# A block up product in the second layer's MLP, the last two groups of the output projection as one product, and the entry's low parts on VectorE

## The chip, the cores and the metric

The kernel runs on one core of one Trainium2 chip. The metric is the device time of one execution in microseconds (us); less is better. The core's engines work side by side, each through its own list of instructions in a fixed order: TensorE (PE in the profile) multiplies, VectorE (DVE), ScalarE (ACT) and GpSimd (POOL) compute on tiles, SyncE (SP) issues the transfers from and to DRAM. An instruction waits for the tiles it reads, and for those it overwrites to be free.

## The reference, cut to what matters

Two layers over 1104 columns (tokens): 1024 new ones, 64 sample ones, 16 meta rows. Layer 0 is a Mamba mixer with eight groups and an MLP; layer 1 is sliding-window attention and an MLP, which no longer need the meta rows (1088 columns).

```
def rmsnorm(x, w):
    return x * lax.rsqrt(jnp.mean(x * x, axis=-1, keepdims=True) + EPS) * w

def sq_relu_mlp(h, norm_w, w_up, w_down):        # 1024 -> 4096 -> 1024
    return h + jnp.square(jax.nn.relu(rmsnorm(h, norm_w) @ w_up)) @ w_down

# layer 0
h = h + gated_group_rmsnorm(y, z, gate_w) @ w_out        # w_out: 2048 -> 1024
h = sq_relu_mlp(h, mlp_norm_w[0], w_up[0], w_down[0])
# layer 1
h = h + attention(h) @ w_o
h = sq_relu_mlp(h, mlp_norm_w[1], w_up[1], w_down[1])
y = rmsnorm(h, final_norm_w)
```

## The kernel before

**Precision.** Every float32 operand of a matmul is split into a high part (a cast to float32r on ScalarE) and a low part (the difference). A product of 128 by 128 weights is three matmuls (`mm3`: L151 high by high, L152 high weights by low activations, L153 low by high). `wunit` loads weights and splits them: cast L136 on ScalarE, low part L137 on GpSimd, and with `pre` a scaling L134 on GpSimd before.

**Columns** are handled in three chunks of one PSUM bank: 384, 384 and 336 (`CH`), in the second layer 384, 384 and 320 (`CH1`). Activations lie feature by partition: eight tiles u (or k) of 128 features. `S` holds the high and low parts of the eight tiles.

**Layer 0, end of the mixer.** `gate_group(g)` makes the gated and normed output of group g, `down` multiplies it by `w_out[g]` and adds the product to the stream `hh` (L695), group after group. In the last group the chunks are finished one by one in the order 0, 2, 1, and `done` of `entry` squares each pair of tiles (L769, sums L772, L775) and, after the last, takes the norm: the statistic is a matmul with ones (`sum_over`, cast `msh` L194, low part `msl` L195, matmuls L196 and L197), Ln and Exp on ScalarE (L205, L206), eight scalings (L782), eight casts (L783), eight low parts (L784), every other one on GpSimd.

**Layer 0, up product.** The 32 weight columns tiles are 16 pairs. Pair 0 is multiplied plainly (`plain_up`). For the other 15 the product of two by two blocks is formed with seven products instead of eight (Strassen and Winograd): `up_weights` makes the sums of weight blocks (`s`: L857, L863; their parts L847 on ScalarE, L848 on GpSimd), `sides` makes the differences of activation blocks (L793, in place) and their parts (casts L803, low parts L806 in two halves, one on GpSimd and one on VectorE). Six of the differences' part tiles lie in pool `T`. `up_pair` multiplies in the PSUM banks ma, md, mc, mb, ma, mc, md (`CHAIN`), 24 matmuls of 276 columns each time, joins them (L875) and writes the squared result to DRAM (`r_d`). Three of the eight steps of `sides` are issued ahead of the plain pair.

**Layer 0, down product.** `down_blocks` reads r back in eight blocks of four tiles, each loaded while the one before is multiplied; `parts` splits them (L926, L927). Tiles `hh` are loaded again from `h_d`.

**Layer 1.** Keys, values and queries, 64 attention blocks (scores in PSUM tiles `sc`, of which there are two) and four sample halves, then `out_unit`: product with `w_o`, two residual adds (L1304, L1305), cast (L1306) and low part (L1307) into `S`, squares (L84, sums L85). `finish` takes the three statistics together after the last output. The MLP is `mlp`: weights scaled by the norm's weight (L134), plain products, 24 matmuls per 128 columns of weights and chunk, the norm's factor applied at the eviction (L738). Its result stays in SBUF, four weight columns at a time, and goes straight into the down product.

**The order.** A list scheduler orders all instructions of an engine by a simulated timeline; tile pools with few buffers limit how far one engine runs ahead of another. A weight's raw tile has two buffers, its split parts six.

Of the kernel before, what the change touches and what calls it, by code (L numbers as in the profile page):

```python
# [8 lines left out]
F32 = mybir.dt.float32  # L9
# [7 lines left out]
P = 128  # L17
# [12 lines left out]
G = 8  # L30
# [10 lines left out]
QW = T // 4  # L41
# [3 lines left out]
class Norm:  # L45
# [30 lines left out]
    def squares(self, c, u, h):  # L76

        k, nc, n = self.k, self.k.nc, self.chs[c][1]
        if u == 0:
            self.acc[c] = k.n1("acc")[:, :n]  # L80
            nc.scalar.activation(out=self.acc[c], in_=h, func=AF.Square)
            return
        sq = k.n1("sq")[:, :n]
        nc.scalar.activation(out=sq, in_=h, func=AF.Square)  # L84
        nc.vector.tensor_tensor(out=self.acc[c], in0=self.acc[c], in1=sq, op=ALU.add)  # L85

    def finish(self, order):

        k, nc = self.k, self.k.nc
        self.rs = self.acc  # L90
        mss = {c: k.sum_over(self.rs[c], self.chs[c][1]) for c in order}
        for c in order:
            nc.scalar.activation(out=self.rs[c], in_=mss[c], func=AF.Ln, bias=k.eps1)
        for c in order:
            nc.scalar.activation(out=self.rs[c], in_=self.rs[c], func=AF.Exp, scale=-0.5)

# [16 lines left out]

class Kernel:
# [13 lines left out]
    def wunit(self, view, a, b, pre=None):  # L128
# [6 lines left out]
        wh, wl = (self.wtile([P, a, b]) for _ in range(2))  # L135
# [32 lines left out]
    def more_banks(self, ctx, n, stat=1):  # L168
        pool = self.pool("psx", bufs=n, space=PSUM, ctx=ctx)
        sp = self.pool("pss", bufs=stat, space=PSUM, ctx=ctx)  # L170
        old = self.gring
        self.gring = old + [pool] * n
        self.pstat = (sp, "ms", stat)
# [12 lines left out]
    def sum_over(self, ssum, n):  # L186
# [9 lines left out]
        nc.tensor.matmul(out=ms[:, :n], lhsT=self.ones_r, rhs=hi, start=True, stop=False)  # L196
# [3 lines left out]
    def rstd(self, ssum, n, eps, scale=1.0, rs=None):  # L200

        nc = self.nc
        if rs is None:
            rs = self.n1("rs")[:, :n]
        nc.scalar.activation(out=rs, in_=self.sum_over(ssum, n), func=AF.Ln, bias=eps, scale=scale)  # L205
        nc.scalar.activation(out=rs, in_=rs, func=AF.Exp, scale=-0.5)  # L206
        return rs
# [515 lines left out]
    def mlp(self, layer, hts, chs, mp, xs, tail, done, pre=None, first=None):  # L723
        nc, i = self.nc, self.i
        for fb in range(8):
            rx = {}
            for c in range(len(chs)):
                rh = mp.tile([P, 4, 384], F32R, tag="rh", bufs=3, name="rh")
# [881 lines left out]
```

## Time and profile before

| | |
|---|---|
| median of 3 runs | 3107.47 us (3106.71 to 3111.19) |
| the profiled execution | 3105.48 us |
| its span in the trace | 3103.8 us |
| mean granted clock of TensorE | 0.981 |
| PE busy | 2956.5 us, 18862 matmuls |
| VectorE, ScalarE, GpSimd busy | 1806.4, 1251.5, 1261.7 us |
| DMA | 258.31 MB, mean 83 GB/s |

The page of the profile has the busy time of each engine, the span in 40 slices of 77.6 us with the busy share in tenths, the chain of work that ended last (PE makes 79% of it), and groups of instructions by line. A view of waits says which instruction waited for which and how long; the windows view gives the same busy times for a stretch of the span. Duration of a single matmul includes the overlap with the next one, so the rate of a stage is read from how many start in a window. The stages in time: mixer until about 1080, the first MLP's up product until about 1470, its down product until about 1690, keys, queries and attention until 2288, its last outputs until 2311, the second MLP until the end.

### The profile page before, as it was taken

The page shows a single profiled execution, that of the slowest core. Times are in us where ns is not written, and L with a number is a line of the kernel's source. Part 1 is how long each engine was busy: PE and PEld are TensorE (multiplying, and loading weights), DVE is VectorE, ACT ScalarE, POOL GpSimd, SP SyncE. Part 2 cuts the span into 40 slices and gives each one's busy share as a digit, 9 for nine tenths or more (in the row PEclk, how much of TensorE's full clock was granted, in tenths as well). Part 3 has the DMA queues.
Part 4 walks back from the last instruction along what each step waited for, and adds up shares of the span by engine and source line. Part 5 has one row for each costly group of instructions (what it writes and reads, how often), then busy time and mean ns, then how long its engine had stood idle before and what let it go on. Part 6 is the DMA issues. An engine that isn't in the chain of part 4 may idle for free.

```text
span 3103.8 us, 47669 instructions
## 1 busy us (share of the span) xinstructions
PE 2956.5 (95%) x18862; PEld 2828.9 (91%) x18862; DVE 1806.4 (58%) x3113; ACT 1251.5 (40%) x2425; POOL 1261.7 (41%) x1054
## 2 busy tenths in 40 slices
PE   6999999989999959999999999999979999999998
PEld 4988889879999959999999998888869999999998
DVE  5777777775656684333433356787976543344436
ACT  5455555554544555444211126665642111111113
POOL 4466666653323254444212145575542223222222
PEclk8999999999999979999999999999999999999999
DMA  3244444444212213333422212122111111111111
GB/s 128 67 121 116 119 125 117 131 123 139 66 61 73 99 53 103 110 113 129 170 102 71 77 41 62 63 85 89 62 48 41 46 44 48 42 48 41 48 41 65
DMA packets 165351, 258.31 MB, mean 83 GB/s; under 512 B 25656, under 2 KB 122040, under 8 KB 163064
## 3 DMA queue, kind: packets, MB, share of 16 engines
q1 hardware_dynamic: 165128, 255.27, 26.4%
q8 instruction: 148, 2.42, 0.3%
q14 instruction: 75, 0.61, 0.1%
HBM read 207.55 MB, written 48.63 MB: 83 GB/s over the span
## 4 chain that ended last, share of the span: by engine, by line
PE 79%; DVE 10%; ACT 4%; issue 3%; POOL 2%; DMA 2%; SPq 0%; DVEq 0%; POOLq 0%; ACTq 0%
PE g L152 20%; PE g L151 20%; PE g L153 20%; PE y L565 1%; PE mc L153 1%; PE mc L151 1%; PE mc L152 1%; PE md L152 1%; PE md L153 1%; PE md L151 1%; PE ma L151 1%; PE ma L152 1%; PE ma L153 1%; PE y L569 1%; DMA dcol<-in_a_d_skip_dram 1%
## 5 line engine op out<-in xcount | busy, mean ns | idle before, releaser
L137 POOL TENSOR_TENSOR w<-raw,w 128x1024 fp32r<-128x1024 f32 x214 | 518.0, 2421 | 1067.1 <-ACT w L136 1011.3
L151 PE MATMUL g<-S,w 128*128 128x384 f32 (+2 forms) x2760 | 923.0, 335 | 6.4 <-DVE kvf L1020 2.1
L152 PE MATMUL g<-S,w 128*128 128x384 f32 (+2 forms) x2760 | 926.1, 336 | 3.0 <-DVE S L288 3.0
L153 PE MATMUL g<-S,w 128*128 128x384 f32 (+2 forms) x2760 | 920.3, 333 | 0.0
L151 PEld LDWEIGHTS g<-S,w 128*128 128x128 f32 x2760 | 521.6, 189 | 14.0 <-issue 2.6
L152 PEld LDWEIGHTS g<-S,w 128*128 128x128 f32 x2760 | 522.0, 189 | 10.2 <-DVE S L288 4.0
L153 PEld LDWEIGHTS g<-S,w 128*128 128x128 f32 x2760 | 522.5, 189 | 6.3 <-issue 3.7
L136 ACT CAST w<-raw 128x1024 fp32r<-128x1024 f32 x214 | 224.1, 1047 | 698.2 <-PE g L152 613.3
L695 DVE TENSOR_TENSOR hh<-hh,g 128x384 f32<-128x384 f32 (+1 forms) x384 | 197.6, 532 | 227.2 <-PE g L153 226.9
L153 PE MATMUL g<-rh,w 128*128 128x384 f32 (+1 forms) x768 | 250.7, 326 | 0.0
L152 PE MATMUL g<-rl,w 128*128 128x384 f32 (+1 forms) x768 | 250.6, 327 | 0.0
L151 PE MATMUL g<-rh,w 128*128 128x384 f32 (+1 forms) x768 | 249.8, 327 | 0.0
L695 DVE TENSOR_TENSOR hf<-hf,g 128x384 f32<-128x384 f32 (+1 forms) x168 | 88.6, 531 | 196.1 <-PE g L153 195.9
L503 DVE SCALAR_TENSOR_TENSOR fm<-xp,cv,fm 128x1024 f32<-128x1024 f32 x96 | 164.5, 1714 | 31.0 <-ACT fm L484 30.4
L134 POOL TENSOR_TENSOR raw<-raw,nv 128x1024 f32<-128x1024 f32 x60 | 118.1, 1969 | 144.0 <-DMA raw<-in_w_up_dram 104.9
L741 DVE TENSOR_TENSOR r<-r 128x384 f32<-128x384 f32 (+1 forms) x96 | 113.1, 1179 | 62.3 <-ACT rh L740 62.2
L153 PEld LDWEIGHTS g<-rh,w 128*128 128x128 f32 x768 | 144.2, 188 | 0.0
L152 PEld LDWEIGHTS g<-rl,w 128*128 128x128 f32 x768 | 144.2, 188 | 0.0
L151 PEld LDWEIGHTS g<-rh,w 128*128 128x128 f32 x768 | 143.9, 188 | 0.0
L740 ACT ACTIVATE rh<-r 128x384 fp32r<-128x384 f32 (+1 forms) x96 | 48.5, 506 | 219.8 <-DVE r L738 219.8
L848 POOL TENSOR_TENSOR w<-s,w 128x512 fp32r<-128x512 f32 x60 | 81.2, 1358 | 133.0 <-ACT w L847 133.0
L151 PE MATMUL g<-gh,w 128*128 128x384 f32 (+1 forms) x384 | 126.7, 332 | 2.2 <-DVE gt L667 1.1
(388 smaller groups left out, 6392.5 us busy)
## 6 DMA issues: line engine op xcount, KB each, us to landing
raw<-in_w_up_dram SPq DMA_DIRECT2D x64, 512.0 KB
raw<-in_w_down_dram SPq DMA_DIRECT2D x64, 512.0 KB
raw<-in_w_in_dram SPq DMA_DIRECT2D x48, 512.0 KB
ab<-acs_d SPq DMA_DIRECT2D x64, 256.0 KB
raw<-in_w_q_dram SPq DMA_DIRECT2D x24, 512.0 KB
raw<-in_w_o_dram SPq DMA_DIRECT2D x24, 512.0 KB
S<-r_d SPq DMA_DIRECT2D x20, 552.0 KB
r_d<-rx SPq DMA_DIRECT2D x15, 552.0 KB
```

Source lines behind the costliest of these rows:

```text
L134: nc.gpsimd.tensor_tensor(out=raw, in0=raw, in1=pre, op=ALU.mult)
L136: nc.scalar.copy(out=wh, in_=raw)
L137: nc.gpsimd.tensor_tensor(out=wl, in0=raw, in1=wh.bitcast(F32), op=ALU.subtract)
L151: mm(out=out, lhsT=wh, rhs=xh, start=(first and k == 0), stop=False)
L152: mm(out=out, lhsT=wh, rhs=xl, start=False, stop=False)
L153: mm(out=out, lhsT=wl, rhs=xh, start=False, stop=(k == n - 1))
L503: nc.vector.scalar_tensor_tensor(out=acc[:, :SEQ], in0=xp[:, k:k + SEQ], scalar=cv[:, j, k:k + 1], in1=acc[:, :SEQ], op0=ALU.mult, op1=ALU ...
L565: nc.tensor.matmul(out=y[64 * h:64 * h + 64, j, :n], lhsT=xdt[:n, 2 * j + h, :], rhs=dec[:n, 2 * j + h, :n], start=True, stop=True)
L695: nc.vector.tensor_tensor(out=hv, in0=hv, in1=pt[:, :n], op=ALU.add)
L740: nc.scalar.activation(out=rx[c][0][:, f, :n], in_=r[:, :n], func=AF.Square)
L741: nc.vector.tensor_tensor(out=r[:, :n], in0=r[:, :n], in1=r[:, :n], op=ALU.mult)
L848: nc.gpsimd.tensor_tensor(out=t[:, 1], in0=src, in1=t[:, 0].bitcast(F32), op=ALU.subtract)
```

## The change

1. **Second layer.** `mlp`, `Norm.squares` and `Norm.finish` go. A new class `Stream` takes the output of the attention: it writes the stream to DRAM (`h_e`), sums the squares, and takes the statistic of chunks 0 and 2 as soon as they are complete, among the attention blocks, in a tile of the `sc` ring. After the attention the stream is read back into a tile `X` of 1088 columns and normed in place; chunk 1 goes into `X` directly and is normed after the first plain product of pair 0. Pair 0 is multiplied plainly from the unnormed parts in `S` with pre-scaled weights. `sides` takes its differences from `X`, in temporary tiles for the first and third block; the other 15 pairs go through `up_pair` with blocks of 272 columns, r goes to DRAM (`r_e`), and the down product reads it back in eight blocks as in the first layer.
2. **Mixer's end.** Groups 6 and 7 of `w_out` are one product of four inner tiles, made chunk by chunk in the order 0, 1, 2; half of its weights lie in a pool of their own (`wx`). Chunk c−1 is normed after four tiles of chunk c, chunk 2 after the first product of the plain pair. The statistic's matmul is kept in program order there (`pin`).
3. **Parts.** The low parts of the entry and of `sides` are all made on VectorE, in one instruction instead of two halves. All steps of `sides` in the first layer now follow the plain pair.
4. The order of the down product's buffers in the first layer alternates between the halves of `S`.

The diff, cut:

```
+class Stream:
+    def place(self, c, u, n):
+        return self.k.n1("hs")[:, :n] if self.X is None else self.X[:, u, self.cols(c)]
+    def done(self, c, u, h):
+        nc.sync.dma_start(out=self.h_d[:, u, self.cols(c)], in_=h)
...
+        if u == KT - 1 and self.X is None:
+            k.pstat = (self.ps, "sc", 2)
+            self.rs[c] = k.rstd(self.acc[c], n, k.eps1, rs=self.acc[c])
+    def load(self, X):
+        for c in self.rs:
+            self.k.nc.sync.dma_start(out=X[:, :, self.cols(c)], in_=self.h_d[:, :, self.cols(c)])
+        for c in list(self.rs):
+            self.norm(c)
+    def norm(self, c):
+        if c not in self.rs:
+            self.rs[c] = k.rstd(self.acc[c], self.chs[c][1], k.eps1, rs=self.acc[c], pin=True)
+        for u in range(KT):
+            nc.vector.scalar_tensor_tensor(out=x, in0=x, scalar=self.w[:, u:u + 1], in1=self.rs[c], ...)
...
-                (nc.gpsimd if k % 2 else nc.vector).tensor_tensor(out=xl[:, k], in0=x, in1=xh[:, k].bitcast(F32),
-                                                                  op=ALU.subtract)
+                nc.vector.tensor_tensor(out=xl[:, k], in0=x, in1=xh[:, k].bitcast(F32), op=ALU.subtract)
...
+        def step(i, k):
+            t = b11 if temps is None else temps[k]
...
+            nc.scalar.copy(out=hi, in_=src)
+            nc.vector.tensor_tensor(out=lo, in0=src, in1=hi.bitcast(F32), op=ALU.subtract)
...
-                for g in range(G):
-                    if g + 1 < G:
-                        gx.append(list(self.gate_group(g + 1, xs))[-1])
-                    self.down(self.i["w_out"][g], 2, gx[g], hts, CH,
-                              2 if g == G - 1 else 0, done if g == G - 1 else None, order=(0, 2, 1))
+                for g in range(G - 2):
+                    gx.append(list(self.gate_group(g + 1, xs))[-1])
+                    self.down(self.i["w_out"][g], 2, gx[g], hts, CH)
+                ws = [self.wunit(self.i["w_out4"][v], 4, 256, to=more) for v in range(2)]
+                gx.append(list(self.gate_group(G - 1, xs))[-1])
+                ws += [self.wunit(self.i["w_out4"][v], 4, 256) for v in range(2, 4)]
+                for c, (o, n) in enumerate(CH):
+                    x = [gx[G - 2][c][e] + gx[G - 1][c][e] for e in range(2)]
+                    for u in range(KT):
+                        self.down_unit(ws[u // 2], 4, u % 2, u, c, n, x, hts, done)
+                        if c and u == 3:
+                            norm(c - 1)
...
+                    next(plain)
+                    norm(2)
+                    for _ in plain:
+                        pass
+                for i in (1, 2, 3, 5):
+                    for k in range(2):
+                        step(i, k)
...
+            stream.load(self.pool("X", ctx=cx).tile([P, KT, META], F32, name="X"))
+            for e in outs:
+                self.out_unit(*e)
...
+                for i in (1, 2, 3):
+                    step(i, 0)
+                next(plain)
+                stream.norm(1)
+                for i in (1, 2, 3):
+                    step(i, 1)
+                for _ in plain:
+                    pass
+                for i in (0, 4, 5, 6):
+                    for k in range(2):
+                        step(i, k)
+            cb.close()
+            cx.close()
+            R0 = self.pool("R0", ctx=cx).tile([P, 2, 4, META], F32R, name="R0")
+            self.up(1, rd, R0)
...
+            for u in range(KT):
+                nc.sync.dma_start(out=big[:, u], in_=h_d[:, u])
+            bufs = [R0] + self.halves(META) * 4
+            self.down_block(1, rd, 0, bufs, hts, chs)
+        for b in range(1, 8):
+            self.down_block(1, rd, b, bufs, hts, chs, 2 if b == 7 else 0, ...)
```

Three places in the order of the engines, with the lines of each kernel. First VectorE at the end of the mixer in the kernel before, from the last adds into the stream on (`acc`: sums of squares, `s`: sums of weights, `S` and `T`: low parts):

```order
L775 TENSOR_TENSOR acc<-acc,n_11149 128x336 x2
L195 TENSOR_TENSOR msl<-acc,msh 128x336
L863 TENSOR_TENSOR s<-s,raw 128x512
L772 TENSOR_TENSOR acc<-n_11205 128x384
L775 TENSOR_TENSOR acc<-acc,n_11227 128x384
L782 SCALAR_TENSOR_TENSOR hh<-hh,nv,rs 128x336 x8
L775 TENSOR_TENSOR acc<-acc,n_11227 128x384
L784 TENSOR_TENSOR S<-hh,S 128x336
L793 TENSOR_TENSOR hh<-hh 128x4x276
```

And the same place now, from the last add on:

```order
L724 TENSOR_TENSOR hh<-hh,g 128x336
L778 TENSOR_TENSOR acc<-acc,n_11226 128x336
L786 SCALAR_TENSOR_TENSOR hh<-hh,nv,rs 128x384 x8
L778 TENSOR_TENSOR acc<-acc,n_11226 128x336
L863 TENSOR_TENSOR s<-raw 128x512 x2
L788 TENSOR_TENSOR S<-hh,S 128x384 x8
L222 TENSOR_TENSOR msl<-acc,msh 128x336
L869 TENSOR_TENSOR s<-s,raw 128x512
L786 SCALAR_TENSOR_TENSOR hh<-hh,nv,rs 128x336 x8
L788 TENSOR_TENSOR S<-hh,S 128x336 x2
L795 TENSOR_TENSOR hh<-hh 128x4x276
```

Before, chunks 2 and 1 (336 and 384 columns) were summed and normed behind the last add. Now only the second norm of 384 columns and that of chunk 2 stand there, with all eight low parts of a chunk, and the first differences stand behind chunk 2.

Second, VectorE at the start of the second MLP. Before, the statistics follow the last output (`hs`), and the first evictions `r` follow them:

```order
L1307 TENSOR_TENSOR S<-hs,S 128x384
L85 TENSOR_TENSOR acc<-acc,sq 128x384
L195 TENSOR_TENSOR msl<-acc,msh 128x384
L195 TENSOR_TENSOR msl<-acc,msh 128x320
L195 TENSOR_TENSOR msl<-acc,msh 128x384
L738 SCALAR_TENSOR_TENSOR r<-g,acc 128x384
```

Now, behind the statistic of chunk 1, the eight scalings of that chunk, four evictions of the plain pair (L835) and thirteen passes of 1088 columns (differences L795, parts L818) stand ahead of the first sums of weights (`s`); the end of that piece (`t`: the temporary tiles, `R0`: the part of the first down block):

```order
L818 TENSOR_TENSOR T<-t_22935,T 128x1088
L835 SCALAR_TENSOR_TENSOR n_23135<-g,acc 128x384
L835 SCALAR_TENSOR_TENSOR n_23164<-g,acc 128x384
L818 TENSOR_TENSOR T<-X,T 128x1088
L795 TENSOR_TENSOR t_22935<-X,t_22935 128x1088
L818 TENSOR_TENSOR T<-t_22935,T 128x1088
L795 TENSOR_TENSOR t_22935<-X,t_22935 128x1088
L818 TENSOR_TENSOR S<-t_22935,S 128x4x272
L863 TENSOR_TENSOR s<-raw 128x512 x2
L945 TENSOR_TENSOR R_23193<-R_23193 128x1088
```

The sums of weights, which the second block product and the later ones need, come last; in the first layer two of them stand ahead of the parts of chunk 1, as the piece above shows.

Third, PE among the attention blocks, at the place where the statistic of chunk 0 stands now (`g<-S`: queries, `sc`: scores):

```order
L179 MATMUL g<-S,w 128x384
L223 MATMUL ms<-msh,ones_r 128x384
L1219 MATMUL sc<-kb,qs 32x128 x4
L1221 MATMUL sc<-ks_18053,qs 128x80
L177 MATMUL g<-S,w 128x384
L178 MATMUL g<-S,w 128x384
L179 MATMUL g<-S,w 128x384
L226 MATMUL ms<-msl,ones_r 128x384
```

Before, all three statistics stood behind the last output product:

```order
L196 MATMUL ms<-msh,ones_r 128x384
L197 MATMUL ms<-msl,ones_r 128x384
L196 MATMUL ms<-msh,ones_r 128x320
L197 MATMUL ms<-msl,ones_r 128x320
```

So two of them moved up among the scores, with 72 query matmuls of 320 columns and 21 of 384 in one run just ahead of the first. On SyncE's queue the stores into `h_e` and two loads into `X` are new, and at the start of the second down product the loads of the next block's r stand ahead of the eight loads of `hh` from `h_e`.

More of the change, by code (lines that the diff above doesn't have):

```diff
@@ L1289, in attention, with out_unit @@
                 half, sp = 0, None
[L1290 to L1294 removed]
+        return outs
+    def out_unit(self, c, n, pr, v, a, xs, stream):
         nc = self.nc
```

337 lines of the change are left out of this document (167 added, 170 removed).

## The prediction

> **What bounds the kernel now.** The first page of the profile comes first: it says which engine sets the time.
>
> ```profile
> span 3103.8 us, 47669 instructions
> PE 2956.5 (95%) x18862; PEld 2828.9 (91%) x18862; DVE 1806.4 (58%) x3113; ACT 1251.5 (40%) x2425; POOL 1261.7 (41%) x1054
> PE   6999999989999959999999999999979999999998
> ```
>
> PE is busy 95% of the span. So there are two ways to get faster: fewer matmul columns, or less idle PE, and the idle PE sits in a few slices of the second view (a 5 in the 15th, a 7 in the 31st). The stretches around these slices, and one of each steady stage, come from the windows view (columns: length, busy time and instructions of each engine, then the granted clock, the DMA share and GB/s).
>
> ```profile
> 1080.00:1122.00 42.00, 3.90 (x17) 2.93 (x15) 39.17 (x50) 21.14 (x34) 20.41 (x14) 0.59 0.10 34
> 1122.00:1180.00 58.00, 55.51 (x364) 55.03 (x364) 39.53 (x37) 32.95 (x54) 31.84 (x21) 0.94 0.25 79
> 1200.00:1300.00 100.00, 100.00 (x790) 100.00 (x789) 36.21 (x44) 47.62 (x82) 43.85 (x35) 1.00 0.34 109
> 1500.00:1600.00 100.00, 100.00 (x598) 100.00 (x597) 36.32 (x58) 17.35 (x16) 21.11 (x9) 1.00 0.26 91
> 2063.00:2112.00 49.00, 45.33 (x333) 39.77 (x332) 41.00 (x85) 26.60 (x72) 30.64 (x23) 0.93 0.31 95
> 2260.00:2288.00 28.00, 21.57 (x156) 16.76 (x155) 20.06 (x51) 13.46 (x39) 10.19 (x10) 1.00 0.13 38
> 2288.00:2346.00 58.00, 44.36 (x218) 41.22 (x217) 33.36 (x40) 24.80 (x37) 15.93 (x7) 0.85 0.11 37
> 2330.00:2340.00 10.00, 8.76 (x35) 8.46 (x36) 1.20 (x3) 8.94 (x12) 0.00 (x0) 0.66 0.00 0
> 2400.00:2600.00 200.00, 200.00 (x1211) 200.00 (x1210) 87.83 (x135) 29.25 (x41) 58.10 (x26) 1.00 0.13 44
> ```
>
> The two holes are the entry to the first MLP (1080 to 1180) and the entry to the second (2288 to 2346). What PE waits for there is in the view of waits, first over 960 to 1190, then over 2250 to 2420:
>
> ```profile
> PE ms L196 <- ACT msh L194: 38.1, 2, 22.8
> PE mc L151 <- DVE rx L875: 2.5, 1, 2.5
> ...
> PE g L151 <- DVE hs L1304: 11.1, 5, 5.6
> ```
>
> Entry one: 42.0 − 3.9 + 58.0 − 55.5 = 40.6 us idle, and 6% of 58 us at the lower clock, 3.5: **44 us lost**, nearly all before a statistic's matmul. Entry two: 58.0 − 44.4 = 13.6 idle and 34% of 10 us: **17 us lost**, behind VectorE's residual adds.
>
> **A, the block product in the second layer.** It removes 2304 plain matmuls (32 × 3 × 24). In their stage PE never waits; 1211 in 200 us make 165.2 ns each (columns 384, 384, 320): 380.5 us. It adds 144 plain ones, 23.8 us, and 15 × 168 of 272 columns. The same product in the first layer runs 790 in 100 us with PE at 100%, at 276 columns:
>
> ```profile
> L151 PE MATMUL ma<-S,w 128*128 128x276 f32 x72 | 20.8, 289 | 0.0
> ```
>
> 126.6 ns × 272/276 = 124.8, times 2520 = 314.4 us. **A = 23.8 + 314.4 − 380.5 = −42 us.** The sums of weights, the evictions and the DRAM traffic it adds hide under PE as in 1200 to 1300 (other engines below 48%, DMA 0.34); the down product then reads its input from DRAM as at 1500 to 1600, where PE also stands at 100%. If this cover failed by 2%, it would cost 6 us.
>
> **B, the first entry.** The groups of 1080 to 1122 (VectorE, then GpSimd, then ScalarE) show why it was long:
>
> ```profile
> L782 DVE SCALAR_TENSOR_TENSOR hh<-hh,nv,rs 128x384 f32<-128x384 f32 (+1 forms) x16 | 14.2, 956 | 2.9 <-ACT rs L206 2.9
> L775 DVE TENSOR_TENSOR acc<-acc,n 128x384 f32<-128x384 f32 (+1 forms) x10 | 8.9, 891 | 0.1
> L784 DVE TENSOR_TENSOR S<-hh,S 128x384 fp32r<-128x384 f32 (+1 forms) x8 | 4.6, 606 | 0.0
> L857 DVE TENSOR_TENSOR s<-raw 128x512 f32<-128x512 f32 x2 | 1.3, 676 | 0.0
> L772 DVE TENSOR_TENSOR acc<-n 128x384 f32<-128x384 f32 x1 | 0.6, 551 | 0.0
> ...
> L784 POOL TENSOR_TENSOR S<-hh,S 128x384 fp32r<-128x384 f32 (+1 forms) x8 | 9.7, 1223 | 8.9 <-ACT S L783 8.9
> L806 POOL TENSOR_TENSOR T<-hh,T 128x552 fp32r<-128x552 f32 x3 | 5.6, 1876 | 5.2 <-ACT T L803 5.2
> L848 POOL TENSOR_TENSOR w<-s,w 128x512 fp32r<-128x512 f32 x1 | 1.3, 1264 | 4.8 <-ACT w L847 4.8
> ...
> L803 ACT CAST T<-hh 128x1104 fp32r<-128x1104 f32 x3 | 3.3, 1112 | 5.7 <-DVE hh L793 5.7
> L205 ACT ACT_TABLE_LOAD x2 | 2.6, 1283 | 0.0
> L847 ACT CAST w<-s 128x512 fp32r<-128x512 f32 x1 | 0.6, 603 | 0.0
> ```
>
> All three chunks end together, so the norms stand one behind the other while PE has nothing. After the change chunks 0 and 1 are squared and normed inside the joint product. Counted from its last matmul, in the new order of VectorE: the last eviction and square sums 1.6, eight norm steps of chunk 1 at 0.6, ScalarE's cast 0.5: the last statistic can start at 7, and PE has 24 plain matmuls (384 columns at 174.5 ns = 165.2 × 384/362.7, so 4.2 us): 3 us idle. Then 72 more cover 12.6 us, against 7.7 to the statistic's second half, 3.7 for Ln and Exp with two table loads, 4.8 of norm steps and the first part: again about 1 idle, and the eight steps of chunk 2 are paced by VectorE (eight parts at 0.55 and two differences, 7 us) against 3.7 on PE: 5 to 7 more. The block differences, all eight now behind the plain pair, come 1.5 late. Sum 12, and with the lower clock behind the gaps 3 more: **15 us lost instead of 44, B = −29**. Bounds: 8 (the parts keep pace) and 25 (gate 7, which lost its cover by group 6, and work queued on VectorE shift the start by 6, and GpSimd's weight parts stretch the rest). The 24 evictions that the joint product saves, about 13 us of VectorE, lie beside PE and count as nothing.
>
> **C, the second entry.** Groups of 2287 to 2346 (three of VectorE, two of GpSimd), and a 1104-wide part of the first layer:
>
> ```profile
> L1307 DVE TENSOR_TENSOR S<-hs,S 128x384 fp32r<-128x384 f32 x8 | 10.0, 1256 | 4.9 <-ACT S L1306 4.8
> L1305 DVE TENSOR_TENSOR hs<-hs,S 128x384 f32<-128x384 f32 x8 | 7.9, 984 | 0.2
> L1304 DVE TENSOR_TENSOR hs<-g,S 128x384 f32<-128x384 f32 x8 | 4.4, 550 | 0.9 <-PE g L153 0.9
> ...
> L137 POOL TENSOR_TENSOR w<-raw,w 128x1024 fp32r<-128x1024 f32 x4 | 9.5, 2384 | 21.4 <-ACT w L136 21.4
> L134 POOL TENSOR_TENSOR raw<-raw,nv 128x1024 f32<-128x1024 f32 x3 | 6.4, 2144 | 1.4 <-DMA raw<-in_w_up_dram 1.4
> ...
> L927 DVE TENSOR_TENSOR S<-S 128x1104 fp32r<-128x1104 f32 x4 | 5.2, 1305 | 2.0 <-ACT S L926 2.0
> ```
>
> Here the new order of VectorE is long. From the last 57 output matmuls on it has, ahead of chunk 1's statistic, 31 passes of 0.55 (17.0), sixteen norm steps (9.0), six differences or parts of 1.30 (7.8) and one eviction: 35 us, and 5 for GpSimd beside it (8 adds of L1307 took 10.0 instead of 4.4): the statistic at 41, when PE, with 141 matmuls, has been out of work since about 25. Then 24 plain matmuls and Ln, Exp: 49. Behind them on VectorE: eight norm steps 4.5, four evictions 2.2, thirteen 1.30 passes 16.9, about 3 waiting for ScalarE's casts: 75. And only then come the first sums of weights (in the first layer they stood ahead of the differences), so PE's second block product waits for all of this: sum 0.7, a cast of 1.1 for the first down block and its load, which ScalarE has in front, 0.6, GpSimd 1.3: 79. Six products of 24 × 124.8 ns follow, 18 us, and 2 at the lower clock: 99. PE's own work in that stretch is 165 × 174.5 ns, 48 × 145.5 and 168 × 124.8: 57. So 42 us are lost instead of 17, **C = +25**. Bounds: 0 (the evictions and differences run in the shade of attention after all) and +35 (GpSimd doubles more of the passes).
>
> **D, attention.** The statistics of chunks 0 and 2 now sit among the score matmuls and take one of the two score buffers, and 93 query and output matmuls run ahead, where they no longer cover blocks. An uncovered stretch lost 28.0 − 21.6 = 6.4 us (2260 to 2288), a covered one 3.7 of 49. Six blocks of about 5 us uncovered cost some 5, the wait for the statistic up to 4, the second place 3: **D = +10**, between 0 and 18.
>
> **E, the start of the second down product.** Eight loads of the next block are issued ahead of the eight loads of the stream, 4.4 MB each, at about 400 GB/s, as the first layer's loads ran:
>
> ```profile
> GB/s 0 0 16 25 225 407 406 327 380 393 367 411 420 414 406 424 422 414 409 304 344 384 426 433 389 402 415 424 411 379 361 399 406 418 394 135 33 0 0 0
> ```
>
> The first piece of the stream then lands some 13 us late, and seven PSUM banks of 12 matmuls cover 7 × 12 × 166 ns = 14: **E = +1**, 0 to 4. The buffers' other order in the first layer costs nothing: PE is full there.
>
> Sum: −42 − 29 + 25 + 10 + 1 = −35. The profiled execution took 3105.5 (span 3103.8), 2.0 under the median of 3107.5. 3105.5 − 35 = **3070.5, forecast 3071**.
>
> **Two rules beside this.** The windows show the clock at 0.59 and 0.66 around the gaps, 3.5 us lost each time. The Trainium skill, "TensorE: Matmul & The Clock Gate", on HAM oscillation, says that an idle window of about 3.4 us puts PE to half speed until it has been busy as long; by that each of my three gaps above that length costs 1.7 us, 5 in all, what the sum has. The trace agrees in kind. The rows above show eight adds of 0.55 us taking 1.26 beside GpSimd. The Trainium skill, "SBUF — State Buffer", on who interferes with whom, says that a VectorE instruction with two SBUF inputs is locked out while GpSimd reads; by that the entry could lose GpSimd's whole 11 us instead of the 5 taken: 3077.
>
> **Rivals.** (1) *The second entry stays hidden*: C is 0, the rest stands: 3046. For it: X is loaded early and half the norming is ready before the last output group. Against: the order of the sums behind the differences. (2) *The entries eat the product*: C +35, D +18, E +4, B only −19: 3105.5 − 42 − 19 + 57 = 3101; with half of it 3086. For it: VectorE is busy 41 of the 49 us from 2063 on already. (3) *Slower*: the score buffer. With one of two held, a block's scores wait for the softmax of the one before; a block of 5 us becomes one of up to 10. Without D the sum is −45; the sixteen blocks of both stretches at 3.2 us more each make 51, and from there on the change is slower by over 6 us; at 5 us each it ends at 3140. Against: the statistic's own chain (cast, two matmuls, Ln) is some 3 us long. (4) *The block product does not run at its first-layer rate*, say each matmul at 140 ns: A = −4, 3109, no change. Nothing in the profile speaks for it.
>
> **Chances and range.** Forecast (3059 to 3080) 0.55; rival 1 (3040 to 3058) 0.19; rival 2 (3080 to 3101) 0.20, of which 0.03 ends within 0.2%; rival 3 0.04, rival 4 0.02. 0.2%, 6.2 us, is about what a measurement of this kernel can tell from no change. Faster 0.91, same 0.05, slower 0.04. The range 3045 to 3094 leaves out the far ends of rivals 1 and 2, and 3 and 4.
>
> **What would show it.** A: 2520 matmuls of 272 columns at 125 ns, PE full from the second pair on. B: two waits of 3 to 7 us at the first entry and none of 20. C: PE's wait for the statistic near 14 us and one of 20 or more before the second block product, ended by ScalarE or GpSimd on the weights. If that second wait is missing, rival 1 holds; if PE waits longer than 8 us on scores, D is wrong.

## The result, and the profile after

| | before | after |
|---|---|---|
| median | 3107.09 us (3106.06 to 3111.19, 4 runs) | 3082.98 us (3081.20 to 3084.41, 4 runs) |
| ratio, 95% interval | | 0.992 [0.9902, 0.9937] |
| span of the profiled execution | 3103.8 us | 3081.9 us |
| matmuls, bytes moved | 18862, 258.31 MB | 19222, 305.87 MB |

The change makes the kernel 24 us faster; the forecast was 36. The time lies inside the range of the prediction (3045 to 3094) and outside the forecast's own band (3059 to 3080).

The page of the changed kernel, its first lines and the slices of PE and of its clock:

```profile
span 3081.9 us, 49051 instructions
PE 2929.1 (95%) x19222; PEld 2796.9 (91%) x19222; DVE 1751.6 (57%) x3008; ACT 1377.2 (45%) x2606; POOL 1253.1 (41%) x1079
PE   6999999989999989999999999999987999999998
PEclk8999999999999999999999999999998999999999
```

The 5 in the 15th slice has become an 8: the first entry no longer stands still. In the second half an 8 and a 7 (30th and 31st slice) stand where the single 7 was: the second entry has become longer. The windows view of the two entries and of the two block products (PE, PEld, VectorE, ScalarE, GpSimd, then clock, DMA share, GB/s):

```profile
1080.00:1160.00 80.00, 65.70 (x403) 63.02 (x401) 64.56 (x87) 44.43 (x71) 28.58 (x12) 0.94 0.23 75
1160.00:1200.00 40.00, 36.98 (x289) 36.76 (x290) 20.52 (x20) 19.12 (x32) 19.14 (x13) 1.00 0.42 138
1200.00:1300.00 100.00, 100.00 (x790) 99.90 (x789) 36.07 (x45) 50.08 (x85) 44.23 (x34) 1.00 0.34 110
2275.00:2375.00 100.00, 67.50 (x387) 64.64 (x388) 79.44 (x100) 45.50 (x67) 26.53 (x16) 0.83 0.24 83
2400.00:2600.00 200.00, 200.00 (x1591) 200.00 (x1590) 71.45 (x87) 95.35 (x161) 87.30 (x68) 1.00 0.34 109
```

First entry: 14.3 + 3.0 us idle and 6% of 65.7 at the lower clock, 3.9: 21 us lost. Second entry: 32.5 idle and 17% of 67.5, 11.5: 44 us lost, with VectorE busy 79 of 100 us. The second layer's block product runs at the rate of the first one, with PE full.

PE's waits in the changed kernel, first over 960 to 1190 (total, times, longest):

```profile
PE mc L178 <- DVE T L818: 4.8, 2, 2.8
PE g L177 <- DVE hh L724: 4.3, 2, 3.8
PE md L177 <- DVE rx L882: 2.6, 1, 2.6
PE g L223 <- ACT msh L221: 2.6, 1, 2.6
PE g L178 <- DVE S L788: 2.0, 2, 1.6
PE ms L226 <- DVE msl L222: 1.5, 1, 1.5
PE ma L177 <- ACT rx L908: 1.3, 1, 1.3
PE ms L223 <- ACT msh L221: 1.2, 2, 0.7
```

then over 2250 to 2450:

```profile
PE ma L177 <- DVE n L835: 13.8, 1, 13.8
PE md L177 <- ACT w L853: 6.8, 1, 6.8
PE g L178 <- DVE S L1322: 4.7, 2, 2.4
PE g L177 <- DVE X L1319: 4.5, 2, 4.3
```

and over 2600 to 3090, where the prediction had expected next to nothing:

```profile
PE g L177 <- DVE hh L724: 6.8, 1, 6.8
```

In the first entry, two waits of together 38.1 have become a dozen, in the eight groups above, of which the longest is 3.8; the second entry waits for VectorE's evictions and the weights; and the second down product now begins with a stop.

**Where the time went.** Three matmuls stand at the same place of the program in both kernels: the one of the gates' last common statistic, the first of attention and the last of attention. Their rows in the timeline of the kernel before (start, duration, line) are

```profile
729.19 0.34 PE L196 MATMUL ms<-msh,ones_r 128*128 128x384 f32 x1
1912.98 0.27 PE L1153 MATMUL yb<-ident,es 128*32 128x128 f32 x1
2286.87 0.40 PE L1173 MATMUL yb<-pb,vt 128*64 128x128 f32 x4
```

and in the timeline of the changed one

```profile
731.76 0.34 PE L223 MATMUL ms<-msh,ones_r 128*128 128x384 f32 x1
1898.71 0.27 PE L1170 MATMUL yb<-ident,es 128*32 128x128 f32 x1
2274.60 0.40 PE L1190 MATMUL yb<-pb,vt 128*64 128x128 f32 x4
```

With a second trace of each kernel (the first and the last run below) the stretches between them are, in us:

| stretch | before | after | difference of the means |
|---|---|---|---|
| start to the gates' statistic | 729.2, 730.4 | 731.8, 733.3 | +2.7 |
| from there to attention | 1183.8, 1187.0 | 1167.0, 1166.7 | −18.6 |
| attention | 373.9, 370.8 | 375.9, 374.0 | +2.6 |
| last outputs and second MLP | 816.9, 816.8 | 807.3, 806.1 | −10.1 |
| span | 3103.8, 3105.0 | 3081.9, 3080.1 | −23.4 |

Most of the gain lies in the stretch with the first entry. The second MLP, which saved 40 us of product, kept 10.

### The profile page after: what moved, and what is told of

It reads as the page before. It is cut to its first block, busy times and chain, and to the rows that moved or that the text cites. A ratio compares the mean times of both kernels' runs of the same rounds, so it can differ in the third digit from the quotient of the medians.

```text
span 3081.9 us, 49051 instructions
## 1 busy us (share of the span) xinstructions
PE 2929.1 (95%) x19222; PEld 2796.9 (91%) x19222; DVE 1751.6 (57%) x3008; ACT 1377.2 (45%) x2606; POOL 1253.1 (41%) x1079
## 2 busy tenths in 40 slices
DMA packets 189761, 305.87 MB, mean 99 GB/s; under 512 B 27528, under 2 KB 137480, under 8 KB 187464
## 4 chain that ended last, share of the span: by engine, by line
PE 49%; DVE 8%; ACT 3%; issue 3%; POOL 1%; DMA 1%; SPq 0%; DVEq 0%; ACTq 0%; POOLq 0%
PE g L178 9%; PE g L177 9%; PE g L179 9%; PE md L179 2%; PE md L178 2%; PE md L177 2%; PE mc L179 2%; PE mc L178 2%; PE mc L177 2%; PE ma L177 2%; PE ma L179 2%; PE ma L178 2%; PE mb L179 1%; PE mb L178 1%; PE mb L177 1%
## 5 line engine op out<-in xcount | busy, mean ns | idle before, releaser
L163 POOL TENSOR_TENSOR w<-raw,w 128x1024 fp32r<-128x1024 f32 x184 | 445.9, 2424 | 933.1 <-ACT w L162 866.3
L724 DVE TENSOR_TENSOR hh<-hh,g 128x384 f32<-128x384 f32 (+2 forms) x552 | 287.5, 532 | 445.0 <-PE g L179 444.3
L854 POOL TENSOR_TENSOR w<-s,w 128x512 fp32r<-128x512 f32 x120 | 166.3, 1390 | 332.3 <-ACT w L853 332.3
L854 POOL TENSOR_TENSOR w<-raw,w 128x512 fp32r<-128x512 f32 x90 | 123.1, 1369 | 95.1 <-ACT w L853 64.5
L177 PE MATMUL ma<-S,w 128*128 128x276 f32 (+1 forms) x480 | 139.7, 291 | 15.1 <-DVE n L835 13.8
L179 PE MATMUL ma<-S,w 128*128 128x276 f32 (+1 forms) x480 | 139.4, 290 | 0.0
L178 PE MATMUL ma<-S,w 128*128 128x276 f32 (+1 forms) x480 | 139.1, 290 | 0.0
L177 PE MATMUL g<-gh,w 128*128 128x384 f32 (+1 forms) x384 | 126.9, 332 | 2.4 <-DVE gt L696 1.1
L178 PE MATMUL g<-gl,w 128*128 128x384 f32 (+1 forms) x384 | 126.6, 330 | 0.0
L179 PE MATMUL g<-gh,w 128*128 128x384 f32 (+1 forms) x384 | 126.2, 330 | 0.0
L585 ACT ACTIVATE dec<-ab,acs 128x128 f32<-128x128 f32 (+1 forms) x288 | 90.8, 387 | 67.8 <-PE y L594 64.3
L177 PEld LDWEIGHTS ma<-S,w 128*128 128x128 f32 x480 | 91.1, 190 | 15.7 <-DVE n L835 14.1
L630 POOL TENSOR_TENSOR yt<-yt,yo 128x256 f32<-128x256 f32 (+1 forms) x72 | 68.2, 948 | 88.6 <-DVE yt L627 82.2
```

The costliest lines, as they stand in the source:

```text
L163: nc.gpsimd.tensor_tensor(out=wl, in0=raw, in1=wh.bitcast(F32), op=ALU.subtract)
L177: mm(out=out, lhsT=wh, rhs=xh, start=(first and k == 0), stop=False)
L178: mm(out=out, lhsT=wh, rhs=xl, start=False, stop=False)
L179: mm(out=out, lhsT=wl, rhs=xh, start=False, stop=(k == n - 1))
L585: nc.scalar.activation(out=dec[:n, h, :n], in_=ab[:n, h, :n], func=AF.Relu, scale=-1.0, bias=self.acs[:n, t, 4 * g + h:4 * g + h + 1])
L630: nc.gpsimd.tensor_tensor(out=yt[:, :, :no], in0=yt[:, :, :no], in1=yo[:, :, :no], op=ALU.add)
```

## The experiments

The first eleven are the changed kernel with no edit, with one or with several, each timed against the kernel before; the last is the kernel before itself. Three groups ran on one chip each: the first four kernels (before: 3107.97 us, 3103.44 to 3111.11), the next four (before: 3107.81, 3102.22 to 3111.70), and the three after them (before: 3108.11, 3104.96 to 3109.70). "Last stretch" is the time from attention's last matmul to the end, in one trace.

**1. The changed kernel again**, as the measure for the others.

> The changed kernel once more, beside the three others on the same chip. Both theories expect 3083 us, 24 less than before.

Measured: 3084.31 us (3081.19 to 3086.22), ratio 0.9923 [0.9911, 0.9935].

**2. The first layer's change alone.** `Stream` and the second layer's blocks go out; `mlp`, `squares` and `finish` of before come back behind the changed first layer.

> The first layer of the changed kernel (joint product of groups 6 and 7, the entry's low parts on VectorE, other down buffers) with the second layer of before. My account of the two traces: the first entry saved 17 us, not the 29 that were forecast, so 3090. The rival, that the entry gave its 29 us and the loss came with the second layer: 3078.

Measured: 3088.24 us (3085.88 to 3094.70), ratio 0.9941 [0.9928, 0.9953]; from attention's last matmul to the end 816.2 us, as before. This is near the account's 3090 and far from the rival's 3078. The first layer's change is worth 19.7 us by the medians, about what the table above has (18.6), and the whole second layer's change only the other 4. Its attention takes 370.4 us, so that the changed one (374.0 and 375.9) costs some 4 more.

**3. Sums of weights early** in the second layer, in a memory of their own beside `T`, where nothing has to be freed for them.

```diff
-            self.ws = self.rx
+            self.ws = ws or self.rx
...
+            ws = self.pool("ws", ctx=cr, right=True)
```

> The changed kernel, with the two tiles for sums of weights in a pool of 4 KB of their own beside T instead of memory that X has to leave first. If the second block product waits for those sums alone, the wait of 6.8 us before it goes and the first pair ends 8 to 11 us earlier: 3073 to 3075. The rival, that the differences themselves set the pace: PE's wait moves to T and the time falls by 2 at most, 3081.

Measured: 3078.92 us (3077.49 to 3080.85), ratio 0.9908 [0.9895, 0.9922]. The last stretch is 805.0 us, 1.7 less than the 806.7 of the changed kernel's mean. PE's waits in this kernel, 2250 to 2450:

```profile
PE ma L177 <- DVE n L835: 17.1, 1, 17.1
```

The medians differ by 5.4 us, but the two intervals overlap. Neither the 3073 to 3075 that were expected nor the rival's 3081 came. The wait for the weights (6.8) is gone, the one for VectorE's eviction, ahead of it, has grown from 13.8 to 17.1, and the one for the statistic from 1.7 to 3.8. So the wait did move to VectorE, as the rival said, though to an eviction and not to `T`: whoever takes the late weights away finds VectorE.

**4. The second stream's tiles beside the weights.** `hh` of the second down product lay in the memory that the block product's `rx` gives back last; with one pool moved it lies where the weight tiles were.

```diff
-            self.ws = self.rx
+            self.ws = self.pool("ws", ctx=cq) if layer else self.rx
```

> The changed kernel, with the weight tiles of the second up product in a pool opened after the one of rx, so that the stream's tile hh overlaps with them and not with rx, which is stored to DRAM last. If the loads of hh came late because they had to wait for that store, they are issued before the loads of r, and PE's wait of 6.8 us goes with the half clock behind it: 7 to 9 us less, 3074 to 3076. The rival, that the bandwidth (8.7 MB at 400 GB/s) or the low parts ahead of the evictions on VectorE set it: the same time within 2 us.

Measured: 3072.61 us (3067.58 to 3074.42), ratio 0.9882 [0.9867, 0.9897]: 11.7 less than the changed kernel beside it; the last stretch is 798.8 us, 7.9 less. SyncE's issues at that place show why. In the changed kernel:

```profile
2669.63 0.80 SPq L939 DMA_DIRECT2D S<-r_e  x2
...
2676.28 0.66 SPq L920 DMA_DIRECT2D r_e<-rx  x1
2678.68 0.33 SPq L939 DMA_DIRECT2D S<-r_e  x1
...
2681.32 8.52 SPq L1555 DMA_DIRECT2D hh<-h_e  x8
```

and with `hh` beside the weights:

```profile
2661.89 4.66 SPq L1555 DMA_DIRECT2D hh<-h_e  x8
...
2681.55 0.52 SPq L920 DMA_DIRECT2D r_e<-rx  x1
```

The loads went out 19 us earlier, ahead of the last store of `rx` and not behind it. The windows view of the changed kernel and then of this one, 2670 to 2700:

```profile
2670.00:2700.00 30.00, 23.24 (x128) 22.92 (x127) 16.66 (x18) 11.22 (x12) 4.91 (x2) 0.89 0.98 372
```

```profile
2670.00:2700.00 30.00, 30.00 (x186) 30.00 (x185) 18.44 (x23) 12.56 (x13) 7.77 (x3) 1.00 0.81 316
```

PE starts 186 matmuls there instead of 128, and no wait is left. The rival, that bandwidth or VectorE's low parts set it whatever the place of `hh`, is refuted. But the edit has also changed VectorE's order. In the changed kernel the first adds into `hh` stand behind all eight low parts (L945) of the next block:

```profile
2687.09 3.90 DVE L945 TENSOR_TENSOR S<-S 128x1088 fp32r<-128x1088 f32 x2 [0.65 <-ACT S L944]
2690.99 3.24 DVE L724 TENSOR_TENSOR hh<-hh,g 128x384 f32<-128x384 f32 x7
```

In run 4 the first add is at 2673.09, and four stand ahead of the first low part (2681.35). How much of the 6.8 us was the late load and how much the add's place behind the low parts isn't separated; both came with the place of `hh` in memory.

**5. Low parts shared with GpSimd again** in the first layer (part 3 of the change undone there).

```diff
-                nc.vector.tensor_tensor(out=xl[:, k], in0=x, in1=xh[:, k].bitcast(F32), op=ALU.subtract)
+                (nc.gpsimd if k % 2 else nc.vector).tensor_tensor(out=xl[:, k], in0=x, in1=xh[:, k].bitcast(F32), ...)
...
+            for h in range(2):
+                h = slice(2 * h, 2 * h + 2)
+                (nc.vector if h.start else nc.gpsimd).tensor_tensor(out=lo[:, h], in0=src[:, h], ...)
```

> The changed kernel with part 3 undone in the first layer: every other low part of the entry, and the first half of each difference's low part, on GpSimd again. If VectorE is what the first entry waits for and GpSimd holds it up anyway, sharing costs: each GpSimd part of 1.2 to 1.9 us blocks VectorE for as long as it saves there, 3085 to 3092. The rival, that the move to VectorE was the mistake in the entry (10 us of parts added to the engine that PE waits for): 3075 to 3081.

Measured: 3092.49 us (3089.78 to 3097.26), ratio 0.9952 [0.9940, 0.9964]: 8 more than the changed kernel (half a us above the range that was expected), and 1177.8 us from the gates to attention instead of 1167. PE's longest wait in the first entry, from its view of waits over 1080 to 1180:

```profile
PE g L177 <- DVE hh L724: 11.2, 1, 11.2
```

So of the first entry's 19 us some 8 to 11 hang on part 3. That GpSimd's blocking alone costs them is not shown, because VectorE's order has changed with the edit. The last eviction, for whose bank PE waits, now stands behind the eight scalings of chunk 1:

```profile
1095.16 7.55 DVE L786 SCALAR_TENSOR_TENSOR hh<-hh,nv,rs 128x384 f32<-128x384 f32 x8 [1.52 <-ACT rs L235]
1102.63 0.49 DVE L724 TENSOR_TENSOR hh<-hh,g 128x336 f32<-128x336 f32 x1
```

In the changed kernel it stands ahead of them (1092.05 and 1095.26), and they take 4.32 us. So some 3.2 us of the wait of 11.2 go with these scalings being slower beside GpSimd, which works from 1096.97 to 1102.30; most of the rest goes with the place of the eviction in the list.

**6. The plain pair's low weight parts on VectorE** in the first layer, so that GpSimd has nothing long to do while chunk 2 is added up.

```diff
-        nc.gpsimd.tensor_tensor(out=wl, in0=raw, in1=wh.bitcast(F32), op=ALU.subtract)
+        (lo or nc.gpsimd).tensor_tensor(out=wl, in0=raw, in1=wh.bitcast(F32), op=ALU.subtract)
```

> The changed kernel with the low parts of the plain pair's weights in the first layer on VectorE, so that no GpSimd instruction of 2.6 us stands beside the last square sums and the last adds into hh. If that instruction caused PE's wait of 3.75 us before the plain pair (two adds took 3.74 us instead of 1.0), the wait falls below 2 and the time by 2 to 4: 3080 to 3082. The rival, that VectorE's queue alone is late: the added 2.2 us of work make it 3084 to 3087.

Measured: 3080.58 us (3080.36 to 3082.62), ratio 0.9915 [0.9902, 0.9928]. From the gates to attention it takes 1165.7, 1.2 less. In the changed kernel VectorE and GpSimd stood so (timelines of both):

```profile
1086.24 0.51 DVE L778 TENSOR_TENSOR acc<-acc,n 128x336 f32<-128x336 f32 x1
...
1087.97 0.49 DVE L724 TENSOR_TENSOR hh<-hh,g 128x336 f32<-128x336 f32 x1
1088.38 3.74 DVE L778 TENSOR_TENSOR acc<-acc,n 128x336 f32<-128x336 f32 x2
1092.05 0.49 DVE L724 TENSOR_TENSOR hh<-hh,g 128x336 f32<-128x336 f32 x1
```

```profile
1087.64 2.63 POOL L163 TENSOR_TENSOR w<-raw,w 128x1024 fp32r<-128x1024 f32 x1 [31.41 <-ACT w L162]
1090.23 1.52 POOL L854 TENSOR_TENSOR w<-raw,w 128x512 fp32r<-128x512 f32 x1
```

Here one add remains beside a GpSimd instruction:

```profile
1088.05 1.22 DVE L163 TENSOR_TENSOR w<-raw,w 128x1024 fp32r<-128x1024 f32 x1
1089.18 0.50 DVE L724 TENSOR_TENSOR hh<-hh,g 128x336 f32<-128x336 f32 x1
1089.60 1.42 DVE L778 TENSOR_TENSOR acc<-acc,n 128x336 f32<-128x336 f32 x1
```

The last eviction, for whose bank PE waits, comes at 1090.94 and not at 1092.05, and PE's wait for it falls from 3.8 to 2.6, not below 2 as expected. That the adds stretch beside GpSimd, and that PE waits for it, is shown. What it costs is not known well: the wait at the statistic right behind has grown from 2.6 to 3.4, the one for `rx` has shrunk from 2.6 to 0.4, the stretch of the trace is 1.2 us shorter and the medians differ by 3.7 with intervals that overlap.

**7. Edits 3 and 4 together.**

> The changed kernel with both memory changes, sums early and hh early. They act on different waits, so the gains add: 3084.3 less 11.7 and less 2 to 5 is 3067 to 3071. If the gain of the early sums was chance, 3072.

Measured: 3070.63 us (3068.57 to 3074.04), ratio 0.9883 [0.9870, 0.9895]; last stretch 795.6 us. Early sums add 2 us (medians) to 3 us (stretch) to edit 4; alone they gave 5.4 and 1.7.

**8. The second entry's norms behind the squares**, on top of 7: the scalings of chunks 0 and 2 are kept behind the last output's sum of squares, so that chunk 1's statistic doesn't stand behind sixteen of them.

```diff
+            if c != 1:
+                k.tc.keep_in_program_order(v)
...
+            stream.norms()
```

> The one with both memory changes, and the norms of chunks 0 and 2 in the second layer kept behind the last output's square sums on VectorE. The statistic of chunk 1 then comes about 15 us earlier. If the second entry is bound by the sum of VectorE's work up to the last difference, only its idle time there (about 8 us between 2275 and 2350) can go: 4 to 8 us less than with both, 3060 to 3066. The rival, that PE's wait for the statistic was a cause of its own: 10 to 14 us less, 3055 to 3059.

Measured: 3059.11 us (3058.18 to 3061.17), ratio 0.9845 [0.9833, 0.9858]; last stretch 784.6, 11.0 less than in 7. PE's view of waits, 2230 to 2420, has one large wait left:

```profile
PE ma L180 <- DVE n L838: 18.8, 1, 18.8
```

The waits for the statistic (3.7 in 7) and for the stream's adds (4.3) are gone, the large one has grown (17.2 in 7), and the windows say what is left: between 2300 and 2335 VectorE is never idle.

```profile
2300.00:2335.00 35.00, 17.70 (x97) 17.37 (x95) 35.00 (x44) 18.53 (x23) 10.00 (x5) 0.74 0.21 72
```

So the order of VectorE was a cause, as the rival said (11.5 us by the medians, for 10 to 14), and what is left stands where VectorE has no gap.

**9. Edit 8 alone**, without early sums and with `hh` where the change put it.

> The order of the second entry's norms alone, with the hh and the weight sums' buffers as in the changed kernel. If the order of VectorE there is a cause of its own, it gives here what it gave beside the two other edits, 9 to 12 us: 3071 to 3074. Rival: without early weight sums the second block product waits for its weights (the 6.8 us of the changed kernel) and takes most of it back: 2 to 6 us, 3077 to 3081.

Measured: 3075.92 us (3072.63 to 3079.05), ratio 0.9896 [0.9883, 0.9910]; last stretch 801.6, 5.1 less than in the changed kernel. This lies between the two theories. PE's wait for the weights has grown:

```profile
PE md L180 <- ACT w L856: 10.0, 1, 10.0
```

10.0 instead of 6.8: alone, a part of what the order gives is handed on to the weights. By the last stretch the order gives 5 us by itself and 11 beside early sums, which by themselves give 2, so that the two edits help each other. By the medians it is 8.4, 11.5 and 5.4, and the gains of runs 3, 4 and 9 add up to that of run 8 (25.5 and 25.2). Whether they give more together than apart therefore stays open.

**10. Chunk 1's norm behind chunk 2's squares** in the first entry.

```diff
-                        if c and u == 3:
-                            norm(c - 1)
+                        if c == 1 and u == 3:
+                            norm(0)
+                norm(1, True)
```

The edit also issues a chunk's eight scalings ahead of its casts and low parts, in all three chunks.

> First entry alone: the eight norm passes of chunk 1 are kept behind the square sums of chunk 2's last output, so that fewer of them stand on VectorE ahead of chunk 2's statistic. If a third of what the first entry still loses is this order (the wait for msh was 2.6 us, the wait for msl 1.5 us, the wait for the differences rx 2.6 us), the span falls by 2 to 5 us against the changed kernel: 3078 to 3081. Rival: chunk 1's differences then come later and the plain pair's successor waits as long as before: within 1 us of the changed kernel, 3082 to 3084.

Measured: 3079.91 us (3077.18 to 3080.65), ratio 0.9908 [0.9894, 0.9921]. From the gates to attention 1163.1 us, 3.7 less: as expected. The wait of 2.6 for the last `msh` is gone, and the waits for `T` and `rx` are 4.3 (3.5 and 0.8) and 1.9 instead of 4.8 and 2.6.

**11. All of it**: 4, 3, 8, 6 and 10.

> All edits together: hh beside the weight tiles, weight sums early, norms of the second entry behind the square sums, low parts of the plain pair on VectorE in the first layer, chunk 1's norm passes behind the square sums in the first entry. The parts of the second layer gave 3059.1; the plain pair's low parts gave 3.7 us alone, the norm pin 0 to 5 us: 3050 to 3056 if they add. Rival: the two edits of the first entry meet the same wait and only one of them counts: 3054 to 3057.

Measured: 3053.64 us (3051.27 to 3054.91), ratio 0.9826 [0.9813, 0.9840]; 54 us under before, 29 to 31 under the changed kernel. From the gates to attention 1159.8 us, 7.0 less than in the changed kernel: both edits of the first entry count, and the rival's common wait is not there.

**12. The kernel before again**, for a second trace.

> The kernel before, unchanged, for a second trace. Of the 21.9 us between the two spans, -2.6 had already been given back at the first matmul of the statistic of the gates (729.19 us before, 731.76 after; 730.35 to 733.31 in five more kernels with the changed first layer), ahead of everything that the diff touches. If that is scatter of the start, this trace has the matmul between 730 and 733 at a span of 3104 to 3107. If the changed kernels are really later there, it stands at 729.2 again within 0.5 us.

Measured: 3106.74 us, one run; the matmul stands at 730.43, the span is 3105.0 us. All twelve traces with the changed first layer lie between 730.35 and 733.31, with a mean of 731.7. So single traces scatter there by 1.2 us with one kernel and by 3.0 with the twelve, and the two ranges meet. The means are 1.9 apart; whether that is more than scatter, two traces of before can't say. It stays open.

## Why the prediction was right, and where it was not

The sum of the five terms was −35. Put together from the runs it is −40 − 19 + 22 + 3 + 8 = −26; with the 2.7 us at the start, which stand ahead of the change, that is the −23 of the spans and nearly the −24 of the medians. That it comes out is no check, because C is taken as what the others leave.

**A, −42 forecast, −40 measured.** 1591 matmuls in 200 us are 125.7 ns each, for 124.8 forecast: 23.8 + 2520 × 0.1257 − 380.5 = −39.9. PE is full from the second pair on, and the cover by the other engines held.

**B, −29 forecast, −19 to −20 measured.** The mechanism was right: no statistic of all three chunks, no wait of 20. The sum was too small at two of its terms. The waits up to the plain pair's end are 3.8 for the bank, 2.6 at the last statistic, 0.7 at the one of chunk 0 and 2.0 for the parts: 9.1, and the prediction's steps for them (3, 1, 5 to 7) make 9 to 11. Their sum was met by chance: the parts cost 2.0 instead of 5 to 7, and the bank, 3.8, stood in no step. Of the two waits of 3 to 7 us that were named as a sign, one came. But "the block differences, all eight now behind the plain pair, come 1.5 late" is wrong: the block products wait 4.8 for `T`, 2.6 for `rx` and 1.3 for a bank, 8.7 in all. And gate 7's lost cover stood only in the bound: over 940 to 1000 PE now waits 1.5 for `msl`, 0.8 for `hh` and 0.4 for `msh`, 2.7 us, where it waited 0.4 before. With 7 and 2.7 more, the 15 us lost become 24 to 25, about what the windows (21) and gate 7 give together. The share of the lost cover was not tried by itself.

GpSimd's weight parts, which the bound had too, were a part of the wait for the bank: 1.2 us (run 6).

**C, +25 forecast, +22 measured.** This was the riskiest count, and its points were met: from the last 57 output matmuls at 2275.4 on, the statistic was forecast at 41 and stood at 39.3, the second block product at 79 and stood at 78.0, the end of the pair at 99 and was at 99.2. (+22 is what A and E leave of the 10.1 us that the last stretch gained; these points, with 57 us of work and 17 lost before, make 25, and the windows, 44 us lost against 17, would make 27.) The form of the waits was other than said. Instead of 14 us at the statistic there are 1.7, and some 9 ahead of it, for adds (4.3 and 0.3) and low parts (2.3 and 2.4). Instead of 20 before the second block product there are 13.8 before the first one, until an eviction, and then 6.8. So the sign "if that second wait is missing, rival 1 holds" was a bad one: it is missing in this form, and C is there. Runs 3 and 9 show that the two waits hang together: in 3 the weights' wait goes and the eviction's grows, in 9 the waits ahead shrink and the weights' grows. VectorE's list sets the pace, as the prediction said. Rival 1, with C at nothing, is refuted.

**D, +10 forecast, +3 to +4 measured.** The stretch of attention takes 374.0 to 377.5 us (mean 375.3) in the eleven traces with the changed second layer and 370.4 to 373.9 (mean 371.7) in the three with the old one. The matmuls of the two moved statistics show no wait of their own. Ahead of score matmuls PE waits 4.8 us in all (1675 to 2275), against 1.6 before, and 3.7 of them stand behind the statistic of chunk 0, between 2085 and 2091. The wait of the outputs for `mb` has doubled:

```profile
PE yb L1183 <- DVE mb L1178: 11.3, 10, 2.0
```

against 5.6 before; but the wait of the same product `yb` for `al` has gone from 5.6 to 0.7, so that the two together are nearly as before (12.0 and 11.2). The condition named for D's failure, over 8 us of waiting on scores, didn't come about, and rival 3 with it. What the uncovered blocks cost, 5 us in the sum, was not measured by itself.

**E, +1 forecast, +8 measured: a wrong step.** "The first piece of the stream then lands some 13 us late" and is then covered by seven banks' 14: this counts SyncE's queue alone. Ahead of the queue stood the memory: `hh` lies where `rx` of the last pair lay, and its loads go out at 2681.32, behind the last store of `rx` at 2676.28. The cover was right: PE runs dry at 2684.8, 14.1 us after its first matmul at 2670.70. But the first add into `hh` comes 20.3 us after it, at 2690.99, behind eight low parts on VectorE. Run 4, which moved one pool, took the wait of 6.8 us away, with the half clock behind it.

So the time fell into the band of rival 2 (3080 to 3101). That rival's B of −19 is what came, but its C, D and E, 35, 18 and 4, are not. Against the forecast B is 10 us short, E 7 and A 2; D and C, forecast 7 and 3 too dear, hid half of that. This cancelling was luck, and C's 3 lie within what single traces scatter.

## What to carry to other kernels

Where a hole is filled by moving work under a product, count what the last wait leaves on the engine that feeds it: in both entries VectorE's list, and not the wait that the profile names, set the time, and the wait moved along it until the order itself was changed (11 us with early weights; without them 5 by the trace and 8 by the medians). A load that replaces data kept on chip needs free memory as well as a free queue: look up which tile lay at its address and when that was last read. And where VectorE and GpSimd both work in a hole, try giving VectorE the whole: here the split cost 8 us, in part because it also put an eviction behind eight scalings. An edit that changes the scheduler's order tests the order with it, as runs 4 and 5 did.

## What the runs showed of the hardware

In the rows of run 6, VectorE's add of two tiles in on-chip memory doesn't slow down beside GpSimd by some factor: the times fit an add that stands still until GpSimd's instruction ends. Two adds took 3.74 us, where one alone takes 0.51, beside two GpSimd instructions of 2.63 and 1.52 that followed each other; one add took 1.42 beside a single one of 1.26 (at 1089.39 on GpSimd in run 6). An eviction just ahead of the two, with one operand in PSUM, took its usual 0.49 while the 2.63 one ran. The Trainium skill, "SBUF — State Buffer", on who interferes with whom, says that a VectorE instruction with two inputs in SBUF contends with a GpSimd instruction that reads SBUF, and that one with at most one such input does not. The rows of run 6 agree with it. The prediction had weighed the rule with all of GpSimd's 11 us at the entry; at this place, where GpSimd had worked for 4 us, PE's wait fell by 1.2.

It is not always VectorE that is held. In the changed kernel, eight low parts with both inputs in on-chip memory took 3.83 us from 1101.12 on, 0.48 each as usual, and beside them GpSimd's subtraction of 128x512, which took 1.26 and 1.52 above, took 4.84:

```profile
1101.68 4.84 POOL L854 TENSOR_TENSOR w<-s,w 128x512 fp32r<-128x512 f32 x1 [9.92 <-ACT w L853]
```

A short wait of PE can cost half speed too, and late. The wait of 2.59 us that ended at 1101.13 is shorter than the 3.4 that the prediction reckoned with. Matmuls of 384 columns behind it started 0.17 to 0.18 us apart, until 1102.62; from 1102.87 to 1106.07 they started 0.32 apart:

```profile
1101.13 0.42 PE L223 MATMUL g<-msh,ones_r 128*128 128x336 f32 x1 [2.59 <-ACT msh L221]
1102.44 0.34 PE L177 MATMUL g<-S,w 128*128 128x384 f32 x1
1102.87 0.53 PE L179 MATMUL g<-S,w 128*128 128x384 f32 x1
```

In run 7 the same wait of 2.59 was followed by no such stretch. So it is not only waits above 3.4 us that cost clock: the first entry has just one of them, 3.75, for which the prediction's reckoning gives 1.7 us, and it lost 3.9.

The kernel before differs between two traces by 3.2 us from the gates to attention (1183.8 and 1187.0) and by 3.1 in attention, with opposite signs, at spans 1.2 apart: a stretch of one trace is not good to better than about 3 us, and smaller differences that come from one trace, as the 1.2 us of run 6 and the 1.7 of run 3, are not settled by it.
